# A transformer trunk on one core: key and value products by stream, and a first unit in a written order

## The chip, the cores and the metric

The kernel runs on one core of one Trainium2 chip. The metric is the device time of one launch in microseconds (us); lower is better. The median of three runs of the kernel before is 2077.16 us (2076.76 to 2080.05).

## The reference

Two layers work on two streams of 256 tokens and 1024 channels each, the latent stream and a context stream. In short:

```python
for i in range(2):
    m  = reshape(silu(c)     @ w_ada[i] + b_ada[i])      # 9 vectors of 1024: shift, scale, gate, ...
    mc = reshape(silu(c_ctx) @ w_ada[i] + b_ada[i])
    x  = x  + 0.5 * m[2]  * swiglu(rmsnorm(x)  * (1 + m[1])  + m[0],  w_gate, w_up, w_down)
    xc = xc + 0.5 * mc[2] * swiglu(rmsnorm(xc) * (1 + mc[1]) + mc[0], w_gate, w_up, w_down)
    h, hc = modulated(x, m[3], m[4]), modulated(xc, mc[3], mc[4])
    # token mixer: keys and values of BOTH streams, queries, windowed and global attention,
    # a gated convolution, sigmoid gates, one output projection; then a second feed-forward step
```

In the last layer only the keys and values of the context stream are needed. All is float32; the result has to be accurate to float32, so each product is made as three products of float32r parts (high by high, high by low, low by high).

## The kernel before

**Products.** Channels lie on the 128 partitions (8 blocks `k` of 128), the tokens of both streams side by side in 512 columns: the latent stream in columns 0 to 255, the context stream in 256 to 511. A weight block of 128x1024 is split by a copy on ACT (`wh`) and a subtraction on DVE (`wl`): `split_w`, L181 to L188, three slots of `wh` and `wl`. `mm_chunk` (L198) makes for each `k` the three products of lines L207, L208 and L209. 512 columns or 256 can be asked for.

**Order of work.** The instructions are put in order when the kernel is built, by a scheduler that takes the program's order as priority and a model of when each one is ready; on the chip each engine then runs its own list strictly in that order. Small steps between products (norms, roots, transposes) wait in a hand-made `Queue` (L30): a step is put there with a lag in model microseconds and is written into the program once so much matmul time has passed (`queue.passed`, L210), or when `queue.finish` asks for it.

**A mixer's beginning** (L701 to L712). Two weight blocks are loaded (each has 128 columns of keys and 128 of values for one of the two attentions `b`). `queue.finish(0)` writes what is left of the latent stream's norm, then come `keys(0, 0)` and `keys(1, 0)`, 24 products of 256 columns each; `queue.finish(1)` writes what is left of the context stream's norm and modulation (`modulate`, L416: DVE, ACT, POOL, ACT, DVE); then `keys(0, 1)`, `keys(1, 1)`; then `values(0)`, `values(1)`, 24 products of 512 columns each. For each pair of `b` and stream the keys go through a chain: sums on PE (L649), DVE (L653), a power on POOL (L656), a spreading copy on DVE (L658), and products on PE again (L666), which are written 2.0 model microseconds after the sums. The key weights are split twice (L702, L707), the value weights once: six splits.

**The first unit** (L1015 to L1090). The first feed-forward step's first 256 columns of the gate and the up weights (`raw0`, two halves each) are multiplied before the usual loop starts. For that the first two adaLN vectors (`a` = 1 scale, `a` = 0 shift) are needed. Their weights, 8 MB, are loaded in 8 transfers of 1 MB (`ada_load`, L219), in the order of the four pieces `kp` of 256 channels: `kp` 0, first half of `raw0`, `kp` 1, second half of `raw0`, `kp` 2, `kp` 3. `ada_part` (L226) multiplies a piece of one vector by silu(c) with PE split into four column groups (64 columns each, L231), DVE turns the result (L238), adds the bias (L240) and scales (L248). With them ACT makes `hh` (L1075), DVE the float32 value (L1076) and `hl` (L1079), and PE the products of two blocks `k` (L1088 to L1090; 12 products of 512 columns for each `k`). `split_half` splits half of a `raw0` weight; the fourth of these needs a slot of `wh` and `wl` that is taken. The program's order is vector, modulation, products, piece by piece, and the scheduler may move the products of one piece behind the vectors of another.

Ahead of it the two streams are loaded, turned by PE (L1034), copied (DVE L1038 for the latent stream, ACT L1040 for the context), squared (ACT L1027), their root taken on POOL and spread by PE (L391), and normed on DVE (L1046).

Of the kernel before, what the change touches and what calls it, by code (L numbers as in the profile page):

```python
# [6 lines left out]
F32 = mybir.dt.float32  # L7
# [7 lines left out]
P = 128  # L15
# [45 lines left out]
def trunk(ctx, tc, x, c, ctxt, c_ctx, w_ada, b_ada, norm_g, ffn_w_gate, ffn_w_up, ffn_w_down,  # L61
# [72 lines left out]
    nc.scalar.activation(  # L134
        out=c32[:, :, 0:2], in_=vb[:, 0:16].rearrange("p (v k) -> p k v", v=2), func=AF.Silu
    )
# [26 lines left out]
    def b_ada_v(i, k0, n):  # L163
        return vl[i][:, k0:k0 + n]
# [54 lines left out]
    def ada_load(pool, i, a, kp):  # L219
# [6 lines left out]
    def ada_part(raw, i, a, kp):  # L226
# [7 lines left out]
        ada_done(i, a, ps, 2 * kp, 2)  # L234

    def ada_done(i, a, ps, k0=0, n=KD):
        tt = small.tile([P, S], F32, tag="t1k", name="ada_t", bufs=2)
        nc.vector.transpose(out=tt[:, :32 * n], in_=ps[:, :32 * n])  # L238
        m = mods[i][:, KD * a + k0:KD * a + k0 + n, :]
        nc.vector.tensor_tensor(  # L240
            out=m, in0=tt[:, :32 * n].rearrange("p (m r) -> p m r", r=32)[:, :, 0:2],
            in1=b_ada_v(i, KD * a + k0, n).unsqueeze(2).to_broadcast([P, n, 2]), op=ALU.add,
        )
        ada_scale(i, a, m, k0, n)
# [90 lines left out]
    def mod_v(i, a, k, v):  # L335
        return mods[i][:, KD * a + k, v:v + 1]
# [39 lines left out]
    def rstd(sums):  # L376

        var = small.tile([P, 2], F32, tag="var", name="var")
        nc.vector.tensor_scalar(
            out=var, in0=sums, scalar1=1.0 / D, scalar2=EPS, op0=ALU.mult, op1=ALU.add  # L380
        )
# [4 lines left out]
        return rr  # L386
# [7 lines left out]
    def norm(v, loose, i, a, h, early=None):  # L394
# [8 lines left out]
        rr = rstd(st[:, 0:2])  # L403
# [196 lines left out]
    def mixer(i, h, streams, tail, early=None):  # L600
# [6 lines left out]
        with tc.tile_pool(name="mix", bufs=1) as mp, tc.tile_pool(name="mixt", bufs=2) as tp:  # L607
# [80 lines left out]
            def values(b):  # L688
                pv = acc()
                mm_chunk(pv, split_w(raws[b], KD, slice(P, 2 * P)), x, 0, KD, KD, slice(0, T))  # L690
                zv = tmp()
                nc.scalar.activation(out=zv, in_=pv, func=AF.Copy)
                queue.put(LAG_SQ, "a", lambda: values_turned(b, zv))

            def values_turned(b, zv):
                tv = aux()
                for t in range(4):
                    nc.tensor.transpose(tv[:, t * P:(t + 1) * P], zv[:, t * P:(t + 1) * P], ident)
                nc.vector.tensor_copy(vt[b].rearrange("p t d -> p (t d)"), tv)

            raws = [load(w_in[i], 0, KD, b * WB) for b in range(2)]  # L701
            ws = [split_w(raws[b], KD, slice(0, P)) for b in range(2)]  # L702
            keys_left = [(b, v) for v in range(2) for b in range(2)]
            queue.finish(0)
            for b in range(2):
                keys(b, 0, ws[b])
            ws = [split_w(raws[b], KD, slice(0, P)) for b in range(2)]  # L707
            queue.finish(1)
            for b in range(2):
                keys(b, 1, ws[b])  # L710
            for b in range(2):
                values(b)  # L712
# [302 lines left out]
    for kp in range(KD // 2):  # L1015
        for a in (1, 0):
            adar[kp, a] = ada_load(xin_p, 0, a, kp)
        if kp < 2:
            load_half(kp)


    junk = xin_p.tile([P, D], F32, name="junk", bufs=1)
    un = []
    for v in range(2):
        ss = xin_p.tile([P, 2], F32, tag="ss", name="ss")
        for t in range(2):
            nc.scalar.activation(out=junk, in_=xin[v][:, t, :], func=AF.Square, accum_out=ss[:, t:t + 1])  # L1027
        for kp in range(KD // 2):
# [12 lines left out]
        bc = spread_rows(rstd(ss))  # L1041
        if v == 0:
            vl.append(transposed_rows(*vl_rows[0], "vl0"))
        for kp in range(KD // 2):
            u = xin_p.tile([P, 2, S], F32, tag="xu", name="xu", bufs=8)
            nc.vector.tensor_tensor(  # L1046
                out=u, in0=xT[:, 2 * kp:2 * kp + 2, v * S:(v + 1) * S],
                in1=bc[:, :S].unsqueeze(1).to_broadcast([P, 2, S]), op=ALU.mult,
            )
            un.append(u)  # L1050
# [4 lines left out]
    def split_half(p, hf):  # L1055
        wh, wl = (
            wsp.tile([P, KD, P], F32R, tag=t, name=t).rearrange("p k f -> p (k f)").rearrange(
                "p (k f) -> p k f", k=4)
            for t in ("wh", "wl")
        )  # L1060
        split_x(wh, wl, raw0[p][:, 4 * hf:4 * hf + 4])
        ws0[p] = wh, wl

    for kp in range(KD // 2):
        for a in (1, 0):
            ada_part(adar[kp, a], 0, a, kp)
        if kp == 1:
            load_rest()
        for v in range(2):
            u = un[v * KD // 2 + kp]  # L1070
            ts = slice(v * S, (v + 1) * S)
            hh, hl = (t[:, 2 * kp:2 * kp + 2, ts] for t in h)
            for e in range(2):
                scale, shift = (mod_v(0, r, 2 * kp + e, v) for r in (1, 0))
                nc.scalar.activation(out=hh[:, e], in_=u[:, e], func=AF.Identity, scale=scale, bias=shift)  # L1075
                nc.vector.tensor_scalar(  # L1076
                    out=u[:, e], in0=u[:, e], scalar1=scale, scalar2=shift, op0=ALU.mult, op1=ALU.add
                )
            nc.vector.tensor_tensor(out=hl, in0=u, in1=hh.bitcast(F32), op=ALU.subtract)  # L1079
        if kp % 2 == 0:  # L1080
            for p in range(2):
                split_half(p, kp // 2)
        for k in (2 * kp, 2 * kp + 1):
            for cc in range(2):
                for p in range(2):
                    wh, wl = (t[:, k % 4, cc * P:(cc + 1) * P] for t in ws0[p])
                    ps = first[cc][p]
                    nc.tensor.matmul(ps, wh, h[0][:, k], start=(k == 0), stop=False)  # L1088
                    nc.tensor.matmul(ps, wh, h[1][:, k], start=False, stop=False)
                    nc.tensor.matmul(ps, wl, h[0][:, k], start=False, stop=(k == KD - 1))  # L1090
# [100 lines left out]
```

## Time and profile before

| What | Value |
|---|---|
| Median of three runs | 2077.16 us |
| The profiled execution's own time | 2079.74 us |
| Its span, first to last instruction | 2077.4 us |
| Mean granted clock of TensorE in the span | 0.997 of full speed |
| PE busy | 2041.7 us (98%) |
| DVE busy | 1403.3 us (68%) |
| ACT busy | 854.9 us (41%) |
| POOL busy | 126.0 us (6%) |
| Mean traffic of the DMA queues | 142 GB/s |

The profile is of one execution. Busy time of an engine is the union of its instructions; matmul ends are modelled, so that the rate of PE is read from the distance between two starts. "A <- B" means that A waited and B ended the wait. The granted clock is 1.00 at 2.4 GHz and 0.50 at 1.2 GHz.

### The profile page before, as it was taken

How to read it: one execution, taken by the hardware profiler on the slowest of the kernel's cores; microseconds unless marked ns; L12 is line 12 of the kernel's file. 1: busy time of each engine (PE TensorE's matmuls, PEld its weight loads, DVE VectorE, ACT ScalarE, POOL GpSimd, SP SyncE). 2: the span in 40 equal slices, each digit the busy share in tenths (PEclk: the TensorE clock that was granted, in tenths of full speed). 3: DMA queues.
4: the chain of work that ended last, by engine and by line, in shares of the span. 5: the costliest groups of instructions: out<-in, count | busy, mean ns of one | idle time of the engine just before them, and what ended most of it. 6: DMA issues, size and time to landing. Idle time of an engine off the chain costs nothing. (4 is left out here: it accounts for less than half of the span.)

```text
span 2077.4 us, 29568 instructions
## 1 busy us (share of the span) xinstructions
PE 2041.7 (98%) x11883; PEld 1755.4 (85%) x11883; DVE 1403.3 (68%) x2174; ACT 854.9 (41%) x1357; POOL 126.0 (6%) x137
## 2 busy tenths in 40 slices
PE   6999999999999999999999999999999999999999
PEld 5888888887777888988888898888889887999998
DVE  4778778667764444677776668778566796667554
ACT  4332222546564233532223254222225577456443
POOL 0000000310000000300000030000003200001000
PEclk9999999999999999999999999999999999999999
DMA  9745554041212333465553327446340432667552
GB/s 316 242 152 193 173 191 139 26 117 54 84 55 68 92 101 118 146 193 162 173 182 123 126 81 229 149 148 220 105 144 26 127 108 87 170 200 231 174 184 73
DMA packets 247765, 295.08 MB, mean 142 GB/s; under 512 B 6708, under 2 KB 228300, under 8 KB 247628
## 3 DMA queue, kind: packets, MB, share of 16 engines
q1 hardware_dynamic: 244812, 288.91, 44.2%
q0 software_dynamic: 2560, 4.20, 1.1%
q8 instruction: 93, 1.52, 0.3%
q14 instruction: 44, 0.36, 0.1%
q10 hardware_dynamic: 256, 0.09, 0.0%
HBM read 287.93 MB, written 1.05 MB: 139 GB/s over the span
## 5 line engine op out<-in xcount | busy, mean ns | idle before, releaser
L207 PE MATMUL acc<-hh,wh 128*128 128x512 f32 (+1 forms) x2208 | 773.3, 351 | 0.8 <-ACT hh L191 0.8
L209 PE MATMUL acc<-hh,wl 128*128 128x512 f32 (+1 forms) x2208 | 769.6, 349 | 2.3 <-DVE wl L185 2.3
L208 PE MATMUL acc<-hl,wh 128*128 128x512 f32 (+1 forms) x2208 | 769.8, 349 | 0.8 <-DVE hl L192 0.8
L184 ACT ACTIVATE wh<-raw 128x1024 fp32r<-128x1024 f32 x328 | 326.2, 997 | 683.2 <-PE acc L208 524.7
L185 DVE TENSOR_TENSOR wl<-raw,wh 128x1024 fp32r<-128x1024 f32 x328 | 375.3, 1146 | 214.2 <-ACT wh L184 211.8
L207 PEld LDWEIGHTS acc<-hh,wh 128*128 128x128 f32 x2208 | 418.9, 190 | 61.1 <-issue 8.6
L209 PEld LDWEIGHTS acc<-hh,wl 128*128 128x128 f32 x2208 | 419.2, 190 | 56.8 <-DVE wl L185 3.1
L208 PEld LDWEIGHTS acc<-hl,wh 128*128 128x128 f32 x2208 | 419.6, 190 | 54.4 <-issue 1.6
L280 DVE SCALAR_TENSOR_TENSOR adac<-adar,c,adac 128x1024 f32<-128x1024 f32 x224 | 280.2, 1282 | 42.8 <-DMA adar<-in_w_ada_dram 42.3
L209 PE MATMUL acc<-gh,wl 128*128 128x512 f32 (+1 forms) x824 | 276.3, 336 | 1.3 <-DVE wl L185 1.3
L207 PE MATMUL acc<-gh,wh 128*128 128x512 f32 (+1 forms) x824 | 277.2, 337 | 0.0
L208 PE MATMUL acc<-gl,wh 128*128 128x512 f32 (+1 forms) x824 | 276.3, 335 | 0.0
L184 ACT ACTIVATE wh<-rawd 128x640 fp32r<-128x640 f32 (+1 forms) x152 | 119.1, 784 | 307.9 <-PE acc L208 296.2
L185 DVE TENSOR_TENSOR wl<-rawd,wh 128x640 fp32r<-128x640 f32 (+1 forms) x152 | 134.8, 889 | 76.3 <-ACT wh L184 76.2
L209 PEld LDWEIGHTS acc<-gh,wl 128*128 128x128 f32 x824 | 156.1, 190 | 18.0 <-DVE wl L185 1.9
L208 PEld LDWEIGHTS acc<-gl,wh 128*128 128x128 f32 x824 | 156.4, 190 | 15.9
L207 PEld LDWEIGHTS acc<-gh,wh 128*128 128x128 f32 x824 | 156.4, 190 | 15.9
L351 POOL TENSOR_TENSOR ssq<-ssq,sq 128x256 f32<-128x256 f32 (+1 forms) x42 | 45.8, 1090 | 1441.7 <-ACT sq L348 1441.7
L575 DVE TENSOR_TENSOR sg<-acc,sg 128x512 f32<-128x512 f32 (+1 forms) x90 | 54.6, 607 | 112.3 <-PE acc L209 108.3
L207 PE MATMUL acc<-slot,wh 128*128 128x256 f32 (+1 forms) x352 | 113.4, 323 | 1.3 <-ACT slot L191 1.3
L209 PE MATMUL acc<-slot,wl 128*128 128x256 f32 (+1 forms) x352 | 113.3, 322 | 0.2 <-DVE wl L185 0.2
L208 PE MATMUL acc<-slot,wh 128*128 128x256 f32 (+1 forms) x352 | 113.2, 322 | 0.0
(185 smaller groups left out, 1858.8 us busy)
## 6 DMA issues: line engine op xcount, KB each, us to landing
adar<-in_w_ada_dram SPq DMA_DIRECT2D x128, 512.0 KB, 3.8
raw<-in_ffn_w_gate_dram SPq DMA_DIRECT2D x43, 1024.0 KB, 9.0
raw<-in_ffn_w_up_dram SPq DMA_DIRECT2D x43, 1024.0 KB, 5.4
rawd<-in_ffn_w_down_dram SPq DMA_DIRECT2D x16, 1536.0 KB, 8.0
raw<-in_w_gate_dram SPq DMA_DIRECT2D x24, 1024.0 KB, 6.6
rawd<-in_ffn_w_down_dram SPq DMA_DIRECT2D x16, 1280.0 KB
raw<-in_w_in_dram SPq DMA_DIRECT2D x16, 1024.0 KB, 5.6
adar<-in_w_ada_dram SPq DMA_DIRECT2D x8, 1024.0 KB, 11.9
```

The costliest lines, as they stand in the source:

```text
L184: nc.scalar.activation(out=wh[:, :kc], in_=raw[:, :kc, cols], func=AF.Copy)
L185: nc.vector.tensor_tensor(out=wl[:, :kc], in0=raw[:, :kc, cols], in1=wh[:, :kc].bitcast(F32), op=ALU.subtract)
L207: nc.tensor.matmul(ps, wh[:, k, :], xh, start=first, stop=False)
L208: nc.tensor.matmul(ps, wh[:, k, :], xl, start=False, stop=False)
L209: nc.tensor.matmul(ps, wl[:, k, :], xh, start=False, stop=last)
L280: nc.vector.scalar_tensor_tensor(out=self.acc[:, v], in0=raw, scalar=c32[:, k, v:v + 1], in1=self.acc[:, v], op0=ALU.mult, op1=ALU.add,)
L351: fold.tensor_tensor(out=ssq[:, ts], in0=ssq[:, ts], in1=sq, op=ALU.add)
L575: nc.vector.tensor_tensor(out=sg[:, ts], in0=ps[1][:, ts], in1=sg[:, ts], op=ALU.mult)
```

## The change

In the mixer the values are made stream by stream, as the keys are: both values of the latent stream come before the context stream is needed, and the four value products have 256 columns. The splits of the value weights are kept for the context stream; those of the keys of `b` = 0 are made anew there.

In the first unit the two vectors of a piece are one product: one tile holds both (`[P, KD, 2, WB]`), loaded in four transfers of 512 KB, each with half of the `k` blocks of one vector; the moving side has 128 columns in place of 64, and DVE turns both at once. `in_turn` gives PE a fixed order by `tc.issue_after`, which lets what is in the block follow the named instruction on that instruction's engine: vectors 0; products of k 0; vectors 1; products of k 1 and 2; vectors 2; products of k 3 and the first weight's of k 4; vectors 3; the rest. The fourth split half gets a slot of its own. A first use of Silu on ACT is put at the very beginning, silu(c) behind the first stream's squares; the copies of the first stream on DVE follow its mean; the norms of pieces 1 to 3 on DVE follow the modulation of piece 0.

```diff
@@ beginning
+    warm = xin_p.tile([P, 2], F32, tag="ss", name="warm")
+    nc.scalar.activation(out=warm, in_=ones[:, 0:2], func=AF.Silu)
...
@@ adaLN vectors
-        raw = pool.tile([P, KD, WB], F32, tag="adar", name="adar", bufs=6)
-        c0 = a * D + kp * WB
-        nc.sync.dma_start(out=raw, in_=w_ada[i][:, c0:c0 + WB].rearrange("(k p) f -> p k f", p=P))
+        raw = pool.tile([P, KD, 2, WB], F32, tag="adar", name="adar", bufs=3)
+        for k0 in (0, 4):
+            for a in range(2):
+                nc.sync.dma_start(
+                    out=raw[:, k0:k0 + 4, a], in_=w_ada[i][
+                        k0 * P:(k0 + 4) * P, a * D + kp * WB:a * D + (kp + 1) * WB
+                    ].rearrange("(k p) f -> p k f", p=P)
+                )
...
-            r4 = raw[:, k].rearrange("p (m j r) -> p j m r", j=4, r=32)
+            r4 = raw[:, k].rearrange("p a (m j r) -> p j a m r", j=4, r=32)
             for j in range(4):
-                nc.tensor.matmul(
-                    ps[32 * j:32 * j + 32, :WB // 4], c32[:, k, :], r4[:, j], start=(k == 0), stop=(k == KD - 1)
-                )
+                m = nc.tensor.matmul(
+                    ps[32 * j:32 * j + 32, :WB // 2], c32[:, k, :], r4[:, j], start=(k == 0), stop=(k == KD - 1)
+                )
...
@@ mixer
-            def values(b):
+            def values(b, v, w):
+                ts = slice(v * S, (v + 1) * S)
                 pv = acc()
-                mm_chunk(pv, split_w(raws[b], KD, slice(P, 2 * P)), x, 0, KD, KD, slice(0, T))
+                mm_chunk(pv[:, ts], w, x, 0, KD, KD, ts)
...
-            ws = [split_w(raws[b], KD, slice(0, P)) for b in range(2)]
+            wk = [split_w(raws[b], KD, slice(0, P)) for b in range(2)]
             keys_left = [(b, v) for v in range(2) for b in range(2)]
             queue.finish(0)
             for b in range(2):
-                keys(b, 0, ws[b])
-            ws = [split_w(raws[b], KD, slice(0, P)) for b in range(2)]
+                keys(b, 0, wk[b])
+            wv = []
+            for b in range(2):
+                wv.append(split_w(raws[b], KD, slice(P, 2 * P)))
+                values(b, 0, wv[b])
             queue.finish(1)
-            for b in range(2):
-                keys(b, 1, ws[b])
-            for b in range(2):
-                values(b)
+            keys(1, 1, wk[1])
+            wk[0] = split_w(raws[0], KD, slice(0, P))
+            values(0, 1, wv[0])
+            keys(0, 1, wk[0])
+            values(1, 1, wv[1])
...
@@ first unit
+        if v == 0:
+            with tc.issue_after(sq.ins):
+                nc.scalar.activation(
+                    out=c32[:, :, 0:2], in_=vb[:, 0:16].rearrange("p (v k) -> p k v", v=2), func=AF.Silu
+                )
+        rr = rstd(ss)
...
             if v == 0:
-                nc.vector.tensor_copy(to, of)
+                with tc.issue_after(rr[1].ins):
+                    nc.vector.tensor_copy(to, of)
...
+        pool, kw = (xin_p, dict(bufs=1)) if (p, hf) == (1, 1) else (wsp, {})
...
+    def in_turn(f, *args):
+        if chain:
+            with tc.issue_after(chain[-1].ins):
+                chain.append(f(*args))
+        else:
+            chain.append(f(*args))
...
+    def first_products(k, p):
+        ws = [[t[:, k % 4, cc * P:(cc + 1) * P] for t in ws0[p, k // 4]] for cc in range(2)]
+        for e, r in ((0, 0), (0, 1), (1, 0)):
+            for cc in range(2):
+                m = nc.tensor.matmul(
+                    first[cc][p], ws[cc][e], h[r][:, k], start=(k + e + r == 0),
+                    stop=(k == KD - 1 and e == 1),
+                )
+        return m
+
+    for p in range(2):
+        split_half(p, 0)
+    in_turn(vectors, 0)
+    end = modulated(0)
+    with tc.issue_after(end.ins):
+        for kp in range(1, KD // 2):
+            for v in range(2):
+                normed(kp, v)
     for kp in range(KD // 2):
-        for a in (1, 0):
-            ada_part(adar[kp, a], 0, a, kp)
         if kp == 1:
             load_rest()
...
+            for p in range(2):
+                split_half(p, 1)
+        in_turn(first_products, 2 * kp, 0)
+        if kp < KD // 2 - 1:
+            if kp < 2:
+                in_turn(first_products, 2 * kp, 1)
+            in_turn(vectors, kp + 1)
+            modulated(kp + 1)
+        if kp >= 2:
+            in_turn(first_products, 2 * kp, 1)
+        for p in range(2):
+            in_turn(first_products, 2 * kp + 1, p)
```

## Rows read from the trace of the kernel before

**Rows 1.** The page's busy times, and its 40 slices for PE and its clock.

```profile
PE 2041.7 (98%) x11883; PEld 1755.4 (85%) x11883; DVE 1403.3 (68%) x2174; ACT 854.9 (41%) x1357; POOL 126.0 (6%) x137
...
PE   6999999999999999999999999999999999999999
...
PEclk9999999999999999999999999999999999999999
```

**Rows 2.** Windows: start:end, length, busy (count) of PE, PEld, DVE, ACT, POOL; clock; DMA.

```profile
18.90:30.00 11.10, 7.49 (x189) 6.01 (x189) 8.31 (x18) 5.14 (x7) 0.00 (x0) 0.85 1.09 349
30.00:40.00 10.00, 7.76 (x151) 5.93 (x150) 4.67 (x12) 2.08 (x4) 0.00 (x0) 1.00 1.09 350
40.00:50.00 10.00, 8.10 (x223) 6.42 (x221) 5.19 (x16) 3.13 (x5) 0.00 (x0) 1.00 1.08 344
50.00:60.45 10.45, 10.36 (x50) 8.47 (x51) 5.14 (x12) 4.29 (x7) 0.00 (x0) 1.00 0.08 24
...
411.80:415.40 3.60, 1.65 (x13) 1.40 (x11) 2.70 (x5) 3.26 (x6) 2.46 (x3) 1.00 0.00 0
415.40:418.80 3.40, 3.15 (x14) 3.06 (x15) 2.85 (x9) 2.40 (x5) 2.80 (x3) 0.50 0.00 0
...
1614.30:1616.90 2.60, 0.74 (x7) 0.57 (x6) 1.70 (x4) 2.21 (x4) 1.65 (x1) 1.00 0.00 0
1616.90:1620.30 3.40, 3.40 (x18) 3.30 (x17) 3.40 (x8) 2.82 (x5) 2.84 (x3) 0.50 0.00 0
```

**Rows 3.** Waits in the first unit (18.9 to 60.45): total, times, longest.

```profile
ACT hh L1075 <- DVE mods L240: 10.6, 3, 5.7
...
PE acc L1088 <- ACT hh L1075: 6.3, 3, 2.7
```

**Rows 4.** Timeline of the first unit: start, length, engine and line; in brackets the wait.

```profile
19.54 1.06 ACT L191 ACTIVATE wh<-raw 128x1024 fp32r<-128x1024 f32 x1 [0.78 <-DMA raw<-in_ffn_w_gate_dram]
...
28.50 1.06 ACT L191 ACTIVATE wh<-raw 128x1024 fp32r<-128x1024 f32 x1 [3.31 <-DMA raw<-in_ffn_w_gate_dram]
...
43.68 2.66 PE L231 MATMUL aux<-adar,c 128*32 128x64 f32 x176
...
50.47 0.25 DVE L238 STREAM_TRANSPOSE ada_t<-aux 128x64 f32<-128x64 f32 x1 [0.49 <-PE aux L231]
...
50.95 2.08 ACT L1075 ACTIVATE hh<-xu,mods 128x256 fp32r<-128x256 f32 x4 [2.68 <-DVE mods L240]
...
53.90 0.69 DVE L1079 TENSOR_TENSOR hl<-xu,hh 128x512 fp32r<-128x512 f32 x1
...
60.22 0.39 PE L1090 MATMUL acc<-hh,wl 128*128 128x512 f32 x1
...
60.45 0.27 PE L124 MATMUL aux<-cst,ri 120*128 120x120 f32 x1
```

**Rows 5.** DMA from 0 to 60 us: traffic in 40 slices of 1.5 us; issues, KB, us to landing.

```profile
GB/s 0 126 323 341 179 300 347 345 359 358 346 349 349 348 348 354 348 350 349 348 352 344 349 350 348 347 366 319 344 351 348 339 351 227 56 0 0 0 0 0
...
adar<-in_w_ada_dram SPq DMA_DIRECT2D x8, 1024.0 KB, 11.9
...
xin<-in_x_dram SPq DMA_DIRECT2D x2, 512.0 KB, 5.2
...
raw<-in_ffn_w_gate_dram SPq DMA_DIRECT2D x2, 512.0 KB, 11.5
```

**Rows 6.** Waits of PE at the first mixer's beginning (405 to 440).

```profile
PE aux L666 <- DVE slot L658: 2.4, 3, 1.9
```

**Rows 7.** Timeline of the first mixer's beginning.

```profile
419.39 0.28 PE L207 MATMUL acc<-hh,wh 128*128 128x256 f32 x1
419.51 0.28 PE L208 MATMUL acc<-hl,wh 128*128 128x256 f32 x1
...
420.50 1.22 DVE L185 TENSOR_TENSOR wl<-raw,wh 128x1024 fp32r<-128x1024 f32 x1
...
421.15 1.06 ACT L184 ACTIVATE wh<-raw 128x1024 fp32r<-128x1024 f32 x1 [2.50 <-PE acc L208]
```

More of the change, by code (lines that the diff above doesn't have):

```diff
@@ new lines, in ada_part @@
+        k0, n = 2 * kp, 2
+        tt = small.tile([P, S], F32, tag="t1k", name="ada_t", bufs=2)[:, :WB // 2]
+        nc.vector.transpose(out=tt, in_=ps[:, :WB // 2])
+        for a in (1, 0):
+            nc.vector.tensor_tensor(
+                out=mods[i][:, KD * a + k0:KD * a + k0 + n, :],
+                in0=tt.rearrange("p (a m r) -> p a m r", a=2, r=32)[:, a, :, 0:2],
+                in1=b_ada_v(i, KD * a + k0, n).unsqueeze(2).to_broadcast([P, n, 2]), op=ALU.add,
+            )
+            ada_scale(i, a, mods[i][:, KD * a + k0:KD * a + k0 + n, :], k0, n)
@@ L378, in rstd @@
         var = small.tile([P, 2], F32, tag="var", name="var")
-        nc.vector.tensor_scalar(
+        mean = nc.vector.tensor_scalar(
             out=var, in0=sums, scalar1=1.0 / D, scalar2=EPS, op0=ALU.mult, op1=ALU.add
@@ L686, in keys_split, with values_turned @@
                         nc.gpsimd.dma_start(out=kk[b][po, j, :], in_=k2[pr, b, :])
[L688 removed]
+            def values(b, v, w):
+                ts = slice(v * S, (v + 1) * S)
                 pv = acc()
[L690 removed]
+                mm_chunk(pv[:, ts], w, x, 0, KD, KD, ts)
                 zv = tmp()
[L692 to L695 removed]
+                nc.scalar.activation(out=zv[:, lat], in_=pv[:, ts], func=AF.Copy)
+                queue.put(LAG_SQ, "a", lambda: values_turned(b, v, zv))
+            def values_turned(b, v, zv):
                 tv = aux()
[L697 removed]
+                for t in range(2):
                     nc.tensor.transpose(tv[:, t * P:(t + 1) * P], zv[:, t * P:(t + 1) * P], ident)
[L699 removed]
+                nc.vector.tensor_copy(vt[b][:, 2 * v:2 * v + 2].rearrange("p t d -> p (t d)"), tv[:, lat])
             raws = [load(w_in[i], 0, KD, b * WB) for b in range(2)]
[L702 removed]
+            wk = [split_w(raws[b], KD, slice(0, P)) for b in range(2)]
             keys_left = [(b, v) for v in range(2) for b in range(2)]
@@ L1037, in trunk, with normed @@
             if v == 0:
-                nc.vector.tensor_copy(to, of)
+                with tc.issue_after(rr[1].ins):
+                    nc.vector.tensor_copy(to, of)
             else:
                 nc.scalar.activation(out=to, in_=of, func=AF.Copy)
-        bc = spread_rows(rstd(ss))
+        spread.append(spread_rows(rr[0]))
         if v == 0:
             vl.append(transposed_rows(*vl_rows[0], "vl0"))
[L1044 to L1050, printed above, removed]
+    def normed(kp, v):
+        if v == 0:
+            un[kp] = xin_p.tile([P, 2, T], F32, tag="xu", name="xu", bufs=4)
+        return nc.vector.tensor_tensor(
+            out=un[kp][:, :, v * S:(v + 1) * S], in0=xT[:, 2 * kp:2 * kp + 2, v * S:(v + 1) * S],
+            in1=spread[v][:, :S].unsqueeze(1).to_broadcast([P, 2, S]), op=ALU.mult,
+        )
+    for v in range(2):
+        normed(0, v)
     first = [[acc() for _ in range(2)] for _ in range(2)]
@@ L1061, in split_half, with vectors, modulated @@
         split_x(wh, wl, raw0[p][:, 4 * hf:4 * hf + 4])
-        ws0[p] = wh, wl
+        ws0[p, hf] = wh, wl
+    chain = []
+    def in_turn(f, *args):
[4 more added lines that the diff above has]
+            chain.append(f(*args))
+    def vectors(kp):
+        return ada_part(adar[kp], 0, kp)
+    def modulated(kp):
+        for e in range(2):
+            k = 2 * kp + e
+            u = un[kp][:, e]
+            for v in range(2):
+                ts = slice(v * S, (v + 1) * S)
+                scale, shift = (mod_v(0, r, k, v) for r in (1, 0))
+                nc.scalar.activation(out=h[0][:, k, ts], in_=u[:, ts], func=AF.Identity, scale=scale, bias=shift)
+                nc.vector.tensor_scalar(
+                    out=u[:, ts], in0=u[:, ts], scalar1=scale, scalar2=shift, op0=ALU.mult, op1=ALU.add
+                )
+            end = nc.vector.tensor_tensor(out=h[1][:, k], in0=u, in1=h[0][:, k].bitcast(F32), op=ALU.subtract)
+        return end
@@ L1064, in trunk @@
+    with tc.issue_after(end.ins):
+        for kp in range(1, KD // 2):
+            for v in range(2):
+                normed(kp, v)
     for kp in range(KD // 2):
-        for a in (1, 0):
-            ada_part(adar[kp, a], 0, a, kp)
         if kp == 1:
             load_rest()
[L1069 to L1079, printed above, removed]
```

43 lines of the change are left out of this document (12 added, 31 removed).

## The prediction

> **What bounds the kernel now.** First the page: PE is busy for 2041.7 of 2077.4 us, and the only slice of the forty that is not full is the first [rows 1]. So whatever takes PE time away, or an idle stretch of PE, moves the end one for one; the other engines (DVE 68%, ACT 41%) matter only where PE waits for them. Then the windows, to find the 36 us in which PE is idle. Three places are touched by the change. In the first unit (18.90 to 60.45 us) PE is idle for 3.61, 2.24, 1.90 and 0.09 us in the four stretches, 7.8 us together, and the clock is 0.85 in the first of them [rows 2]. At the beginning of the first mixer it is idle for 1.95 us (411.80 to 415.40) and then runs 3.40 us at a granted clock of 0.50, which is 1.2 GHz; in the second mixer it is idle for 1.86 us and then has the same 3.40 us at 0.50 [rows 2]. The clock there fell after a stretch in which PE was busy for less than half of the time.
>
> Who ends these waits: in the first unit ACT waits 10.6 us for the vectors from DVE and PE 6.3 us for ACT's `hh` [rows 3]. What is late there is the order on PE itself: the weights of piece 1 are in when the second half of `raw0` is (28.50, behind it in the queue), yet 176 records of vector products stand at 43.68, and the last vectors reach DVE at 50.47 [rows 4]. The transfers are not late: the DMA queue moves about 349 GB/s without a gap from 9 to 49 us [rows 5]. In the mixers it is the key chain (`keys_normed`, L666), which stands in PE's list with nothing ready behind it: 2.4 us in three waits, the longest 1.9 [rows 6].
>
> **The first unit, step by step.** *When the weights are in.* A transfer lands in the order of its issue, and the queue is full. The second half of `raw0` lands at 28.5 [rows 4]; behind it come pieces 2 and 3, 2.1 MB each, at 349 GB/s 6.0 us each: 34.5 and 40.5. Piece 1 lies between the halves: 19.5 + 6.0 = 25.5. The change moves the same bytes in the same order, in sixteen issues for eight; SP is the queue moved through, and what stands behind these on it (constants, weights of the next unit) comes later only if the sixteen take longer. The halves of `raw0` are transfers of 512 KB already: four of them among those of 1 MB leave no dip in the strip, and they land 11.5 us after issue as the others do at 11.9 [rows 5]. I take no delay; a bound from the lowest full slices (319 against 349 GB/s) is 1.1 us over 12 us.
>
> *What the last vectors cost.* 176 records of 64 columns take 2.66 us, 15.1 ns each [rows 4]; a product of float32 is two records, so a piece has 128 of them before, 1.9 us. With 128 columns it has 64. If the columns set the time they cost 30 ns and a piece 1.9 us again; if the record does, 1.0 us. I take 1.9, no gain. Half of it can run before the last half lands: 40.5 + 1.0 + 0.2 for handing over = 41.7.
>
> *What is behind them on PE.* By the written order seven groups of six products follow vectors 3: k 4 (second weight), k 5, 6, 7. A product of 512 columns takes 0.23 us (60.22 to 60.45) [rows 4], so 42 x 0.227 = 9.5 us, and the end would be 51.2. Three groups (4.1 us) cover the modulation of piece 3: from DVE's turn to the first `hh` 0.5 us, the four `hh` in 2.1, the last `hl` done at 54.6, 4.1 us after the turn [rows 4]; what the next group needs (the first block of `hh` and `hl`) is there after some 3 us, with two more small DVE steps counted.
>
> *Whether PE gets there in time.* Before vectors 3 stand nine groups (12.3 us) and two vector pieces (3.8): 16.1 us, from about 21 on (vectors 0 landed, `wh` of the first half from 19.54 [rows 4]) to 40.5. So 3.4 us of waits are free: at vectors 1 for 25.5 and at vectors 2 for 34.5, where the given order makes products that could run wait behind PE. I allow 0.5 us beyond that: end at 51.7 for 60.45, **8.7 us saved**. Best end: 51.2 (9.2). Worst: the 7.8 us of waits stay [rows 2], 3.4 of them free, and one fall of the clock costs 1.7 (half of 3.40): 57.8 (2.6).
>
> *Costed at nothing.* The turn, bias and scale on DVE: four turns of 128 columns for eight of 64; DVE is busy 23.3 and ACT 14.6 us of these 41.6 [rows 2]. The moved Silu, the early first use, the held copies and norms: all before the landing of piece 1, which covers them; without that cover each is worth at most an ACT step of 1.06. The own slot for the fourth half frees its `raw0` buffer earlier, so the next unit's weights land by about 47, before PE wants them.
>
> **The mixers, step by step.** Saved in each: the idle 1.95 and 1.86 us, and half of the 3.40 us at 0.50, 1.7 [rows 2], together 3.6, since between `keys(1, 0)` and `keys(1, 1)` now stand 48 products of the latent stream, 48 x 0.12 = 5.8 us (419.39 to 419.51 [rows 7]), under which the key chain and the context stream's modulation run. Added: four value products of 24 by 256 columns are 96 x 0.12 = 11.5 us, for 48 x 0.227 = 10.9: 0.6. One split less in all, but the third split of `wk[0]` waits for its slot until `keys(1, 1)` is done and has only `values(0, 1)`, 24 x 0.12 = 2.9 us, as cover, for 1.06 on ACT and 1.22 on DVE [rows 7]; queued behind it on ACT are the copies out of PSUM. Between nothing and 1.5 us (two such copies first); I take 0.3, nearest to the bare sum of 2.3. The other two L666 waits, 0.5 us, stay. Net 3.6 - 0.9 = 2.7 each, **5.4 us for two**; bounds 1 and 7.
>
> **Sum.** The profiled execution took 2079.74 us (span 2077.4). 2079.74 - 8.7 - 5.4 = 2065.6. It lies 2.6 above the median of the runs, so the median should come to **2063 us**.
>
> **The rivals.**
>
> *A, the first unit is bound by something else than landing (0.17).* DVE and ACT run their lists in order; if `wh` of the second half stands ahead of `hh` of piece 1 on ACT (as at 28.50 now, after 3.31 us of waiting [rows 4]), everything from there is 2 us late, and a fall of the clock adds 1.7. Saved 5 us: 2067. For it: both were seen here. Against: 3.4 us are free.
>
> *B, the mixers' wait only moves (0.11).* PE comes to `keys(1, 1)` before the last `hl`, or stalls at the third split; 1 us saved for both mixers: 2067.5. For it: in the old order DVE is busy 2.70 of 3.60 and 2.85 of 3.40 us there [rows 2]. Against: 5.8 us of work stand in between.
>
> *C, the written order does not do what it says (0.06).* It orders each engine by itself; the modulations could still come late, as now, and the mixers gain little: 2 + 1 us, 2074.
>
> *D, slower: smaller transfers land later (0.04).* Place: SP's queue, before vectors 3. Price: the two loads of x, 512 KB each with an empty queue, land 5.2 us after issue, of which 1.5 are bytes at 349 GB/s [rows 5]; were the 3.7 us paid by each of the eight added transfers, piece 3 would land 30 us later, the unit end at 81 and the kernel at about 2092. It decides from 14.1 / 8 = 1.8 us for each added transfer on. Against it: the four halves of `raw0` show none of it [rows 5]. The Trainium skill speaks for this rival: "DMA: Bandwidth & Descriptors", section "Measured (HBM→SBUF, 128 partitions, SWDGE, issued from GpSimd)", asks for transfers of at least 1 MiB, and the section "Anatomy of one DMA" gives a fixed cost of about 2.0 us for each; paid in turn, by an estimate from that page, it would be 8 x 2.0 = 16 us, and the gain of 14.1 would turn into a loss of 2. The trace does not agree, as far as a full queue goes: 349 and 350 GB/s in the slices of both pairs of halves, as in those around them [rows 5].
>
> **How the numbers follow.** The forecast has 0.62, A 0.17, B 0.11, C 0.06, D 0.04. A measurement of this kernel can tell about 0.2%, 4.2 us. Forecast, A and B lie below 2073.0: faster 0.90. C is no change: 0.06. D is slower: 0.04. The range takes in the best bounds of both places (9.2 + 7 = 16 below the median, 2061, with 2 us for what comes earlier behind them) and A and B together with a margin: 2059 to 2071.
>
> **What would show it.** In the profile of the changed kernel: the last product of the first unit at 51 to 53 us; L231 records of 128 columns, 256 of them, at about 30 ns; DMA full until about 49 us as now; no window at 0.50 at either mixer's beginning; the L658 wait of 1.9 us gone; PE spacing 0.12 us through values and keys. It would be wrong if the landing of piece 3 came after 42 us, if vectors 3 stood on PE after 44, or if a new wait of over 1 us stood before `keys(1, 1)` or `keys(0, 1)`.

## The result and the profile after

The changed kernel took **2067.35 us** (median of five runs, 2059.93 to 2068.36) against 2078.10 for the kernel before (five runs, the three of 2077.16 among them); the ratio is 0.9937, with a 95% interval of 0.9925 to 0.9949. It is faster by 10.75 us. The forecast was 2063 us, with a range of 2059 to 2071. The profiled execution took 2064.93 us (span 2063.2), which is 14.8 less than the profiled one of before; the forecast of that difference was 14.1.

The page of the changed kernel, busy times and the slices of PE and of its clock:

```profile
PE 2038.1 (99%) x11723; PEld 1757.3 (85%) x11723; DVE 1400.9 (68%) x2172; ACT 851.7 (41%) x1359; POOL 123.5 (6%) x137
...
PE   7999999999999999999999999999999999999999
...
PEclk9999999999999999999999999999999999999999
```

PE is busy for 3.6 us less than in [rows 1] and the span is 14.2 shorter: most of the gain is idle time taken away. The windows of the first unit, in the columns of [rows 2]:

```profile
18.90:30.00 11.10, 8.89 (x81) 6.41 (x82) 9.70 (x20) 5.00 (x8) 0.00 (x0) 0.69 1.09 382
30.00:40.00 10.00, 9.83 (x99) 7.58 (x97) 6.74 (x16) 4.83 (x9) 0.00 (x0) 1.00 1.09 379
40.00:50.00 10.00, 10.00 (x100) 8.00 (x99) 6.26 (x18) 3.03 (x5) 0.00 (x0) 1.00 0.86 273
50.00:60.00 10.00, 10.00 (x46) 8.18 (x45) 7.03 (x14) 5.47 (x8) 0.00 (x0) 1.00 0.59 192
```

The idle 2.24 and 1.90 us of the second and third stage are gone. What is new stands in the first line: the clock is 0.69 there, where it was 0.85, and the queue moves 382 GB/s where it moved 349. The waits of PE up to 60 us and the timeline show what the 0.69 belongs to:

```profile
PE acc L1119 <- ACT hh L1108: 2.5, 1, 2.5
PE acc L1119 <- DVE hl L1112: 0.6, 2, 0.4
PE aux L235 <- DMA adar<-in_w_ada_dram: 0.5, 1, 0.5
```

```profile
17.12 1.08 PE L235 MATMUL aux<-adar,c 128*32 128x128 f32 x32 [0.53 <-DMA adar<-in_w_ada_dram]
18.27 0.32 DVE L240 STREAM_TRANSPOSE ada_t<-aux 128x128 f32<-128x128 f32 x1 [1.90 <-PE aux L235]
18.59 1.06 ACT L190 ACTIVATE wh<-raw 128x1024 fp32r<-128x1024 f32 x1 [2.80 <-DMA raw<-in_ffn_w_gate_dram]
...
19.55 1.08 ACT L1108 ACTIVATE hh<-xu,mods 128x256 fp32r<-128x256 f32 x2
...
20.68 1.22 PE L1119 MATMUL acc<-hh,wh 128*128 128x512 f32 x2 [2.48 <-ACT hh L1108]
26.90 2.00 PE L235 MATMUL aux<-adar,c 128*32 128x128 f32 x64
34.97 1.95 PE L235 MATMUL aux<-adar,c 128*32 128x128 f32 x64
41.18 1.95 PE L235 MATMUL aux<-adar,c 128*32 128x128 f32 x64
...
52.93 0.27 PE L126 MATMUL aux<-cst,ri 120*128 120x120 f32 x1
```

PE is through with vectors 0 at 18.20 and waits 2.48 us for `hh`: 0.8 us for DVE's three steps (done at 18.98), 0.6 because `hh` stands on ACT behind `wh`, and 1.1 for `hh` itself. A stretch at 0.50, 1.2 GHz, begins at 20.22 and lasts 6.83 us. From 20.68 on PE hardly waits, so the unit's end is set by where its products begin and how fast they run. It ends at 52.9 in place of 60.45, 7.5 us earlier.

The mixers, in windows of 20 us from the first sum of the keys on; first two of before, then the same two of the changed kernel:

```profile
410.20:430.20 20.00, 17.28 (x109) 15.30 (x107) 15.31 (x34) 11.63 (x20) 9.51 (x8) 0.91 0.30 83
1612.80:1632.80 20.00, 17.58 (x112) 15.72 (x111) 15.66 (x34) 11.59 (x20) 9.52 (x8) 0.91 0.31 87
```

```profile
402.70:422.70 20.00, 19.29 (x162) 19.05 (x161) 14.84 (x34) 10.49 (x20) 6.90 (x7) 1.00 0.38 105
1603.40:1623.40 20.00, 19.30 (x162) 19.05 (x161) 14.86 (x34) 10.50 (x20) 6.89 (x7) 1.00 0.38 104
```

Idle PE went from 2.72 and 2.42 us to 0.71 and 0.70, and no stretch at 0.50 is left. From the first sum of the keys to the first of the queries the mixers take 48.37 and 37.75 us, where they took 51.88 and 40.98: 3.5 and 3.2 less. So 7.5 + 3.5 + 3.2 = 14.2 us, the whole difference of the spans; what else differs between the two traces nearly cancels: 1.5 us more at 860 us, where a later fall of the clock lasts 6.83 us and in the trace of before 3.41, and 1.8 less around 1850 us, where PE waits for ACT, and ACT for weights of the output projection (`w_o`) to land. The change lies at neither place, and both differ from one trace to the next; the account of the prediction comes back to them.

### The profile page after: what moved, and what is told of

Its sections match the earlier page's. It is cut to its first block, busy times and chain, and to the rows that moved or that the text cites. A ratio compares the mean times of both kernels' runs of the same rounds, so it can differ in the third digit from the quotient of the medians.

```text
span 2063.2 us, 29249 instructions
## 1 busy us (share of the span) xinstructions
PE 2038.1 (99%) x11723; PEld 1757.3 (85%) x11723; DVE 1400.9 (68%) x2172; ACT 851.7 (41%) x1359; POOL 123.5 (6%) x137
## 4 chain that ended last, share of the span: by engine, by line
PE 89%; DVE 3%; ACT 2%; DMA 2%; POOL 2%; issue 1%; SPq 0%; ACTq 0%; POOLq 0%; DVEq 0%
PE acc L206 27%; PE acc L208 27%; PE acc L207 27%; PE aux L874 2%; PE aux L862 2%; PE acc L1119 1%; PE aux L816 1%; DVE wl L184 1%; DMA raw<-in_w_pc_dram 1%; PE aux L819 1%; POOL u L427 1%; ACT wh L183 1%; ACT hh L190 0%; DMA raw<-in_ffn_w_gate_dram 0%; DVE u L422 0%
## 5 line engine op out<-in xcount | busy, mean ns | idle before, releaser
L183 ACT ACTIVATE wh<-raw 128x1024 fp32r<-128x1024 f32 (+1 forms) x326 | 323.8, 997 | 670.8 <-PE acc L207 516.7
L184 DVE TENSOR_TENSOR wl<-raw,wh 128x1024 fp32r<-128x1024 f32 (+1 forms) x326 | 372.2, 1143 | 211.9 <-ACT wh L183 209.9
L206 PEld LDWEIGHTS acc<-hh,wh 128*128 128x128 f32 x2240 | 425.1, 190 | 60.5 <-issue 8.6
L208 PEld LDWEIGHTS acc<-hh,wl 128*128 128x128 f32 x2240 | 425.0, 190 | 54.8 <-DVE wl L184 2.7
L207 PEld LDWEIGHTS acc<-hl,wh 128*128 128x128 f32 x2240 | 425.4, 190 | 52.6 <-issue 1.6
```

Source lines behind the costliest of these rows:

```text
L183: nc.scalar.activation(out=wh[:, :kc], in_=raw[:, :kc, cols], func=AF.Copy)
L184: nc.vector.tensor_tensor(out=wl[:, :kc], in0=raw[:, :kc, cols], in1=wh[:, :kc].bitcast(F32), op=ALU.subtract)
L206: nc.tensor.matmul(ps, wh[:, k, :], xh, start=first, stop=False)
L207: nc.tensor.matmul(ps, wh[:, k, :], xl, start=False, stop=False)
L208: nc.tensor.matmul(ps, wl[:, k, :], xh, start=False, stop=last)
```

## The experiments

The kernel before had medians of 2078.02 us (15 runs) and 2078.07 us (9 runs) beside these kernels.

**Which part gives what: e1_mixer, e2_unit, e3_again.** The kernel before with the mixer's part alone; the changed kernel with the mixer's part undone; the changed kernel once more.

```diff
@@ e1_mixer, on the kernel before
...
+                values(b, 0, wv[b])
             queue.finish(1)
...
+            keys(1, 1, wk[1])
+            wk[0] = split_w(raws[0], KD, slice(0, P))
+            values(0, 1, wv[0])
+            keys(0, 1, wk[0])
+            values(1, 1, wv[1])
@@ e2_unit, on the changed kernel: the same lines back to
...
             for b in range(2):
...
+                keys(b, 1, ws[b])
+            for b in range(2):
+                values(b)
```

> The kernel before with the mixer's part alone. Theory (the two places add up, each by PE idle time and half clock taken away): 6.5 us less than before, 3.5 and 3.2 in the two mixers as the changed kernel's trace shows, no stretch at a granted clock of 0.50 at a mixer's beginning. Rival (the gain of a mixer depends on where the earlier change left the clock and the transfers): less than 3 us, and a new fall of the clock within the next 100 us.

> The kernel before with the first unit's part alone. Theory: the first unit ends at about 53 us in place of 60.45 and the kernel takes 7.5 us less. Rival: the first unit's end hangs on the landing of piece 3, so that at 349 GB/s it ends only at 55 or later and 4 to 5 us are left.

> The changed kernel itself once more, to see what differs from one execution to the next. Theory: the sum of the two parts, 14 us less than before, with 1.7 us more or less for each fall of the clock. Rival: 10 to 11 us less, as the median of its first runs, because something in it is slower than in its profiled execution (the transfers, 380 GB/s there against 349 in the kernel before).

Medians: e1_mixer 2075.68 us (11 runs, 2071.12 to 2079.77; ratio 0.9986, 0.9977 to 0.9995), e2_unit 2070.22 (2068.25 to 2071.66; 0.9960, 0.9947 to 0.9974), e3_again 2065.82 (2063.42 to 2069.03; 0.9939, 0.9926 to 0.9952). In the traces the parts are separate: e1_mixer has both mixers 3.5 and 3.2 us shorter and its first unit ends at 59.9; e2_unit ends it at 51.9 and has the mixers as before, each with its stretch at 0.50. The unit's 8.6 us in the trace of e2_unit are 7.8 in the medians. Of the mixers' 6.7 us in the trace the median of e1_mixer shows 2.3: the rival's number, but without its fall of the clock, since none follows before 868 us. What hides the rest is asked below, in e11_mixer_again. e3_again lies 12.2 us under before, between its theory and its rival; at 380 GB/s again the transfers are not what is slower.

**Transfers of 1 MB: e4_1mb.** The changed kernel with two transfers for a piece in place of four.

```diff
-        for k0 in (0, 4):
-            for a in range(2):
-                nc.sync.dma_start(
-                    out=raw[:, k0:k0 + 4, a], in_=w_ada[i][
...
+        for a in range(2):
+            nc.sync.dma_start(
+                out=raw[:, :, a], in_=w_ada[i][
...
```

> The changed kernel with the adaLN pieces in transfers of 1 MB, two for a piece, in place of four of 512 KB. Theory (the size of the transfers does not count, a full queue hides it): the same time as the changed kernel within 1 us, a little later vectors since no half can run ahead of the landing. Rival 1 (rate of 380 against 349 GB/s comes from the smaller transfers): the queue is back at 349 GB/s and the pieces land later by 2.7 us at piece 3. Rival 2 (smaller transfers cost time each): 1 us or more faster.

2068.04 us (2066.69 to 2068.79); the first unit ends at 56.2, 3.3 us later than in the changed kernel. The median is 0.7 and 2.2 us above the changed kernel's two, and inside the spread of its runs. Its first window, its waits there and the first vectors in its timeline:

```profile
18.90:30.00 11.10, 7.13 (x60) 4.84 (x53) 9.13 (x18) 6.22 (x8) 0.00 (x0) 0.69 1.09 382
```

```profile
PE acc L1118 <- ACT hh L1107: 3.2, 1, 3.2
PE aux L234 <- DMA adar<-in_w_ada_dram: 2.0, 1, 2.0
```

```profile
17.44 1.96 PE L234 MATMUL aux<-adar,c 128*32 128x128 f32 x64 [2.05 <-DMA adar<-in_w_ada_dram]
22.58 0.81 PE L1118 MATMUL acc<-hh,wh 128*128 128x512 f32 x2 [3.19 <-ACT hh L1107]
```

Both sizes move 382 GB/s. What the halves bring is the start: PE runs vectors 0 in one go at 17.44 when the second vector is in, where with halves the first 32 records ran at 15.51, and its first product comes 1.9 us later. Of the other 1.4 us, 1.0 are longer waits for `hl` (1.6 for 0.6). The Trainium skill's page "DMA: Bandwidth & Descriptors", section "Measured (HBM→SBUF, 128 partitions, SWDGE, issued from GpSimd)", asks for 1 MiB or more in a transfer; by that this kernel would have gained. Its rate did not rise, and the unit lost 3.3 us: here, in a full queue that SP and not GpSimd issues to, the trace does not agree.

**Why 380 GB/s: e5_rows, e12_order.** From 19 to 38 us the queue moves 348 to 349 GB/s in all four traces with the first unit of before, and 380 to 389 in all ten with the new one. It is not a rate of the whole kernel: from 40 to 46 us, with the next unit's weights, the changed kernel's queue is as full and moves 350. Two edits ask for its cause: the tile laid out so that each transfer fills one stretch of a partition, and the scale loaded before the shift, as before.

```diff
@@ e5_rows
-        raw = pool.tile([P, KD, 2, WB], F32, tag="adar", name="adar", bufs=3)
+        raw = pool.tile([P, 2, KD, WB], F32, tag="adar", name="adar", bufs=3)
...
-                    out=raw[:, k0:k0 + 4, a], in_=w_ada[i][
+                    out=raw[:, a, k0:k0 + 4], in_=w_ada[i][
...
@@ e12_order
-            for a in range(2):
+            for a in (1, 0):
```

> The changed kernel with the adaLN tile laid out vector by vector ([P, 2, KD, WB]), so that a transfer of 512 KB fills 4 KB in a row in each partition, where the changed kernel's and the 1 MB variant's leave every other KB for the second vector. Theory (the rate of 382 in place of 349 GB/s comes from where the rows land): back at 349 GB/s between 10 and 40 us, piece 3 lands near 40.5, and the first unit ends within 1 us of the changed kernel's 52.4 to 53.0, since PE was not waiting for the landing. Rival (the rate comes from something else, as the number of transfers or their order): 380 GB/s again.

> The changed kernel with the loads of each adaLN piece issued scale first and shift second, as the kernel before has them; sizes, tile and products as changed. Theory (the queue's rate of 380 for 349 GB/s comes from the order in which the two column blocks are read): 349 to 352 GB/s from 19 to 38 us, piece 3 landed at about 40.4 in place of 37.8, and the unit's end at 53 to 54, since products that are ready fill most of the difference. Rival (it comes from where the tiles lie, or from something else of the first unit): 380 GB/s, end 52.4 to 53.0.

e5_rows took 2064.38 us in one run beside 2081.23 of before, e12_order 2067.72 beside 2082.75; their units end at 52.4 and 52.6. First windows of e5_rows and of e12_order:

```profile
18.90:30.00 11.10, 9.58 (x84) 6.92 (x85) 10.03 (x19) 4.62 (x8) 0.00 (x0) 0.69 1.09 381
```

```profile
18.90:30.00 11.10, 9.37 (x83) 6.89 (x84) 9.94 (x19) 4.53 (x8) 0.00 (x0) 0.69 1.09 381
```

Neither the size of the transfers, nor how they land, nor the order of the two vectors makes the rate. The number and the place of the tile's buffers (three of 2 MB for six of 1 MB) were not tried. The cause stays open.

**What the written order brings: e6_free.**

```diff
-        if chain:
-            with tc.issue_after(chain[-1].ins):
-                chain.append(f(*args))
-        else:
-            chain.append(f(*args))
+        chain.append(f(*args))
```

> The changed kernel without the written order on PE: the scheduler places vectors and products by priority and its model; the rest (both vectors in one product, transfers, slots, copies) stays. Theory (the order is what the first unit gains by): products move ahead of the vectors again, the first unit ends at 58 us or later. Rival (the merged vectors and the earlier start are what it gains by): it ends at 54 or earlier.

2070.53 us beside 2081.23; the unit ends at 55.5, between the two expectations. In its timeline the vectors 3 stand in pieces, the last of them at 45.32:

```profile
41.06 0.41 PE L235 MATMUL aux<-adar,c 128*32 128x128 f32 x2
42.17 0.65 PE L235 MATMUL aux<-adar,c 128*32 128x128 f32 x16
43.86 0.64 PE L235 MATMUL aux<-adar,c 128*32 128x128 f32 x14
45.32 1.08 PE L235 MATMUL aux<-adar,c 128*32 128x128 f32 x32
```

So the order on PE is worth 2.5 to 3.1 of the unit's 8 us; about 5 us come with the rest of the new first unit (halves, one turn for both vectors, the fourth slot, the norms held back, the queue's higher rate), which was not taken apart further.

**Two vectors in one product: e7_64col.** Each vector in products of its own, 64 columns, in the same order.

```diff
...
+        for a in (1, 0):
+            ps = aux()
+            for k in range(KD):
+                r4 = raw[:, k, a].rearrange("p (m j r) -> p j m r", j=4, r=32)
+                for j in range(4):
+                    m = nc.tensor.matmul(
+                        ps[32 * j:32 * j + 32, :WB // 4], c32[:, k, :], r4[:, j], start=(k == 0), stop=(k == KD - 1)
+                    )
...
```

> The changed kernel with the two vectors as products of their own again, 64 columns each, in the written order: twice the matmul records and turns. Theory (columns set the time of these products, not their number): the records take 15 ns in place of 30, a piece 1.9 us as before, and the first unit ends within 0.7 us of 52.4 to 53.0. Rival (the number of records sets it): a piece takes 3.8 us, and the first unit ends 5 to 7 us later.

2069.33 us beside 2081.23; the unit ends at 59.2. Its vectors:

```profile
35.59 2.02 PE L237 MATMUL aux<-adar,c 128*32 128x64 f32 x128
41.88 1.92 PE L237 MATMUL aux<-adar,c 128*32 128x64 f32 x121
47.55 0.32 PE L237 MATMUL aux<-adar,c 128*32 128x64 f32 x7 [3.74 <-issue]
```

128 records of 64 columns take 2.02 us, 64 of 128 columns take 1.95: the columns set the time, and side by side gives PE nothing. The 6.3 us that the unit loses (the theory said at most 0.7) have another origin than the rival's: at 23.13 PE has waited 2.10 us for `hl` (0.43 in the changed kernel), within the last vectors it stops for 3.74 us, waiting for nothing that the profile shows but its own issue, and a fall of the clock follows at 48.3. The first unit has 256 records more, and the trace has a packet of an instruction queue between 45 and 46 us; but the changed kernel has one at 45.9 and does not stop. That PE waited for its instructions is a guess, and the cause stays open. The Trainium skill's page "Runtime: NRT & Kernel Launch", section "Instruction fetch mechanics", calls the cost of crossing from one fetched block of instructions to the next mostly hidden; no other trace here has such a stop of over 0.5 us.

**The kernel before again: e8_before.** No edit.

> The kernel before, profiled again, to see which of its stretches at a granted clock of 0.50 come back. Theory (the falls at the two mixers belong to the order there): again one fall at each mixer's beginning, idle 1.9 and then 3.4 us at 0.50; the first unit ends at 60 to 60.5. Rival (they are chance): at least one of the two is missing, and the mixer costs 1.7 us less.

2081.97 us. The mixers' windows, as those shown above:

```profile
411.20:431.20 20.00, 17.90 (x105) 16.40 (x104) 14.83 (x32) 11.66 (x20) 8.79 (x8) 0.83 0.23 62
1616.60:1636.60 20.00, 17.62 (x112) 15.72 (x111) 15.67 (x34) 11.63 (x20) 9.51 (x8) 0.91 0.32 88
```

The falls at the mixers come back, the first of them twice as long (6.83 us). The first unit ends at 61.5, later than expected, with 10.2 us at 0.50 in it where the trace of before has 3.4. In the traces with the old mixer (before, e2_unit, e8_before) all six beginnings have a stretch at 0.50; in the eleven traces with the new one, those below among them, none has. This part of the gain is not chance.

**The mixer's part again: e11_mixer_again.** The kernel of e1_mixer, no further edit.

> The kernel of e1_mixer once more, for a second trace: its eleven timed runs had a median of 2075.7 (2.3 under before) where its trace showed both mixers 6.7 us shorter. Theory (the mixers' gain is there in every execution, and the rest of the difference is half-speed stretches elsewhere that come and go): both mixers 3.5 and 3.2 us shorter than in the kernel before, no stretch at 0.50 there, and stretches at other places that add up with the time: a time of 2076 to 2080 needs two to four more of 3.4 us than the two in the first trace. Rival (in the slower executions the mixers' beginnings themselves lose again): a stretch at 0.50 at one of them, or a wait over 1 us there.

2075.06 us. Both mixers are 3.5 and 3.2 us shorter again, with PE busy 19.27 and 19.30 of 20 us there and no stretch at 0.50. But the old first unit has 10.2 us at 0.50 in this trace (from 23.6 and from 37.3) and 3.4 in that of e1_mixer, and ends at 62.0 for 59.9. So the mixers' gain is there in every trace, and what falls of the clock do to the old first unit moves its end by 2.1 us. A second place works against the gain: the wait for `w_o` around 1850 us costs PE 2.6 us in e1_mixer and 1.9 here, where before and e8_before have 1.3 and 1.1. How much of the 4.4 us that the median of e1_mixer lacks is due to either is not shown, since only the profiled executions can be looked into.

**Filling the wait for `hh`: e9_fill.** The changed kernel with five products behind vectors 0 whose sum is not used.

```diff
+    def fill():
+        for n in range(5):
+            m = nc.tensor.matmul(first[1][1][:, :S], ident, xT[:, n % 2, :S], start=True, stop=True)
+        return m
...
     in_turn(vectors, 0)
+    in_turn(fill)
     end = modulated(0)
```

> The changed kernel with five float32 products of 256 columns (estimated 0.43 us each, 2.1 us) placed on PE between the vectors of piece 0 and the first product, into a sum that the first product starts anew. Theory (the wait of 2.48 us for hh lets the clock fall to 0.50 at 20.2 for 6.83 us, and PE is full from there to the unit's end): the stretch at 0.50 is gone or shorter, first product still at 20.7, end of the first unit 49.5 to 51 in place of 52.4 to 53.0, median 2 to 3 us under the changed kernel's 2066 to 2067. Rival (the clock falls for what PE did before 18 us, not for this wait): stretch and end as before, 52 to 53, median 2066 to 2067. A second rival (the end is set by the landing of piece 3, 37.8, and by vectors 3): the stretch is gone, the waits come back behind vectors 2 or 3, end 51 to 52.

**2062.54 us** (2061.01 to 2063.41; ratio 0.9921, 0.9908 to 0.9935). Windows of its first unit and lines of its timeline:

```profile
18.90:30.00 11.10, 9.59 (x95) 6.93 (x94) 10.64 (x21) 5.70 (x10) 0.00 (x0) 1.00 1.09 381
30.00:40.00 10.00, 9.14 (x94) 6.76 (x93) 6.74 (x17) 3.72 (x7) 0.00 (x0) 1.00 1.09 379
```

```profile
17.68 2.42 PE L1103 MATMUL acc<-xT,cst 128*128 128x256 f32 x10
20.27 0.73 PE L1124 MATMUL acc<-hh,wh 128*128 128x512 f32 x2 [0.16 <-ACT hh L1113]
21.91 0.73 PE L1124 MATMUL acc<-hl,wh 128*128 128x512 f32 x2 [0.92 <-DVE hl L1117]
...
31.35 0.73 PE L1124 MATMUL acc<-hl,wh 128*128 128x512 f32 x2 [0.86 <-DVE hl L1117]
...
40.04 1.96 PE L235 MATMUL aux<-adar,c 128*32 128x128 f32 x64
```

The stretch at 0.50 is gone. In all eight traces of the new first unit without the filler a stretch at 0.50 begins between 19.5 and 23.1 us, in the two with it (e10_lag has it too) none does: it was this wait.

The unit's end is 51.8 and not the 49.5 to 51 of the theory. From its first product to its end the unit takes 32.3 to 32.7 us with 6.83 us at 0.50 (the changed kernel, e5_rows, e12_order), 31.5 and 31.6 with 3.41 (e2_unit, e3_again), and 31.5 and 31.9 with none (e9_fill, e10_lag). At full clock PE runs into waits for `hh` and `hl` (2.2 us between 20.27 and 31.35 here, 0.6 in the changed kernel), which the slow clock had covered. So in the unit the longer fall cost about 0.8 us and the shorter one nothing that shows. The first window of e3_again, with the shorter one:

```profile
18.90:30.00 11.10, 8.30 (x84) 6.33 (x85) 10.30 (x21) 5.69 (x9) 0.00 (x0) 0.85 1.09 382
```

The end is in the range of the second rival, but not by its mechanism: the waits stand behind vectors 0 and 1, and piece 3 was in at 38.0, before vectors 3 at 40.04.

The median is 3.3 us under that of e3_again, and nine of the ten runs of the changed kernel are slower than all five here; the spread is 2.4 us for 9.1. The traces put only 1.1 us (against the changed kernel) and 0.6 (against e3_again) into the first unit. The runs list their granted clock: the ten of the changed kernel have 0.996 to 0.999, the five of e9_fill 0.999 or 1.000. That the clock makes the rest of the gain is likely, but not shown: at 0.996 the changed kernel took 2064.9 to 2069.0 us, and its fastest run, 2059.9, had 0.998.

**The lag of the keys: e10_lag.** e9_fill, and the keys' multiplication put further behind the root.

```diff
-                queue.put(LAG_RSTD, "k", lambda: keys_normed(b, v))
+                queue.put(1.6 * LAG_RSTD, "k", lambda: keys_normed(b, v))
```

> e9_fill and, in both mixers, the keys' multiplication put 3.2 us of PE work behind the root instead of 2.0. Theory (what is left of PE's waits for the keys, 1.9 us in four, is the root on POOL, which comes too soon after its sums): the four waits fall from 1.9 us to under 0.4, each mixer's beginning is 0.7 to 0.9 us shorter than in e9_fill, median 1 to 2 us under it. Rival (the wait only moves, to the next thing that is late, the weights' wl from DVE): the sum of PE's waits in the two stretches stays, median as e9_fill.

**2061.27 us** (2060.67 to 2063.04; ratio 0.9917, 0.9904 to 0.9931), the lowest median of all. Its mixers, and its only wait of PE from 1595 to 1660 us:

```profile
401.40:421.40 20.00, 20.00 (x170) 19.93 (x169) 15.21 (x34) 11.04 (x21) 7.08 (x7) 1.00 0.40 107
1599.40:1619.40 20.00, 20.00 (x170) 19.93 (x169) 15.21 (x34) 11.05 (x21) 7.07 (x7) 1.00 0.39 106
```

```profile
PE aux L816 <- DMA qs<-qs: 0.9, 1, 0.9
```

The waits for the keys are gone, and each mixer is 1.4 us shorter from its first sum of the keys to its first of the queries (0.7 to 0.9 expected); 0.7 of it is the idle time of the window. In the second one 1.2 of it is given back at once, at a new wait of 0.9 us for a transfer of the queries (`qs`). The span is 1.2 us shorter than that of e9_fill, as the medians are (1.3); their runs overlap, so the timing alone does not show it.

## Why the prediction was right, and where it was not

- **Size and sign.** 14.1 us were forecast, the two traces differ by 14.8, the medians by 10.75 and (e3_again) 12.2. The median forecast took it that the changed kernel's profiled run would stand to its median as that of before does, 2.6 us above. It stands 2.4 below: that is the step that failed. The traces show two places, outside what was changed, by which executions of one kernel differ. One is the fall of the clock near 860 us: from the first mixer's first sum to the second's it is 1197.8 us in e3_again, with no fall between; 1199.3 in e9_fill, with 3.41 us at 0.50; 1200.8 in the changed kernel, with 6.83. The other is the wait for `w_o`, here in the changed kernel, in e3_again and in e12_order:

```profile
PE acc L206 <- ACT slot L190: 0.4, 1, 0.4
...
PE acc L206 <- ACT slot L190: 2.4, 1, 2.4
...
PE acc L206 <- ACT slot L190: 2.5, 1, 2.5
```

  It goes up to 3.1 us (e4_1mb). The changed kernel's profiled execution had nearly none of it, where that of before had 1.3, so in this it was a low one. How far these two places make up the 2.4 us is not shown, since the other runs have no trace.
- **First unit, the bound.** Saved 7.5 to 8.6 us over the traces, 8.7 forecast, but not by the forecast's way. The landing was to set the end, with piece 3 in at 40.5 and PE waiting for it. Piece 3 was in at 37.8 (40.4 in the trace of before), since the queue moved 380 GB/s, and vectors 1, 2 and 3 stood on PE at 26.90, 34.97 and 41.18, each later than even the forecast's landings (25.5, 34.5, 40.5). The term that was mis-sized is the work of PE before vectors 3: 16.1 us forecast, 20.5 measured (20.68 to 41.18), with 6.83 us at 1.2 GHz and 0.6 of waits in it. At full clock, in e9_fill, it is 19.8, with 2.2 of waits for `hh` and `hl`, which the forecast had at nothing; the other 1.5 were not traced. The 3.4 us that the forecast held free, as waits at the landings, took up most of the 4.4 by which the term was short: so the number came near, in part by luck. PE bound the unit and not the landing, as in rival A, with `hh` behind `wh` on ACT and a fall of the clock, at piece 0 in place of piece 1; the price was far below A's, since `wh` cost 0.6 us and the fall about 0.8. The queue's higher rate, which nobody forecast, helped the changed kernel at the beginning: `wh` of the first half started at 18.59, for 19.54 in before.
- **First unit, single terms.** The vectors' 1.9 us (measured 1.95; e7_64col) and no delay of landing by the sixteen transfers (e4_1mb: the same rate) held. Half of vectors 3 was to run while the last transfer was still on its way; the whole piece was in when PE came to it, and its 1.95 us stand together. The seven groups behind it took 9.9 us for 9.5. With the unchanged landing rival D fell. Rival C had 2 us saved in the unit; without any written order it is 5 (e6_free).
- **Mixers.** 5.4 us forecast, 6.7 in the traces. The idle time went from 2.72 to 0.71 and from 2.42 to 0.70, the clock stayed at 1.00, and the wait of 1.9 us [rows 6] is gone. The added 0.6 us of columns is there (0.120 us a product for half of 0.227); the 0.3 us for the third split was too high, since no wait for its weights stands before `keys(0, 1)`. The remaining 0.7 us, for both mixers together, was not traced further. What is left of rival B is the 0.7 us wait for the keys, which e10_lag removes.
- **What was named as a sign.** Last product at 52.9 (51 to 53 said), records of 30 ns, no window at 0.50 in the mixers, no new wait over 1 us there: all as said. DMA was full until about 47 us, not 49, by its higher rate.

## What to carry to other kernels

When an idle stretch of the bounding engine is taken out of the middle of a stage, look at its beginning: the wait that is left there can bring a fall of the clock, and a few products of no use in it can keep the clock up (here 2.4 us of filler, 1.1 us of the unit, and a median 3.3 us lower of which the traces explain a part). Do not count half of the slow stretch as the price: waits that the slower clock had covered come up again (6.83 us at 0.50 cost about 0.8 in the unit). Where runs spread by more than the effect sought, lay several traces of one kernel side by side and find the places by which they differ before a median is explained from one trace.

## What the runs showed of the hardware

From 19 to 38 us the queue moved the same weights at 348 to 349 GB/s in one version of the first unit (four traces) and at 380 to 389 in the other (ten), with the engines' share full in both; three edits that should have told the cause did not. A stretch at 0.50 at one place lasts 3.41 us in one execution of a kernel and 6.83 in another (before at 415.4 and e8_before at 415.8), and the one near 860 to 875 us is missing in e2_unit, e3_again and e4_1mb. What such a stretch costs depends on the waits that it covers: near 860 us 3.41 and 6.83 us at 0.50 cost 1.5 and 3.0 us, at the beginning of the first unit nothing that shows and about 0.8.
